# The second SwiGLU half step of a hybrid decoder: gate and up by seven products of block sums, down by pairs of tiles

## The chip, the cores and the metric

One core of a Trainium2 chip runs the whole program. The metric is the device time in microseconds (us) of one execution, as a median of several runs; the trace is that of one profiled execution. The engines are PE (TensorE, the matmuls; PEld its weight loads), DVE (VectorE), ACT (ScalarE), POOL (GpSimd) and SP (SyncE, which issues the DMA transfers here).

## The reference

The program is one step of a decoder layer over 1056 tokens (1024 of a prompt and 8 x 4 samples; 16 meta tokens more are carried through the first part). Of the layer only the end matters here:

```python
h = h + 0.5 * _swiglu(_rmsnorm(h, norm_ffn1), ...)            # first half step
...                                                           # GLA and S5 branches
h = h + merged @ p["w_out"]                                   # output projection
h = h + 0.5 * _swiglu(_rmsnorm(h, p["norm_ffn2"]), w_gate, w_up, w_down)   # second half step
# _swiglu(x) = (silu(x @ w_gate) * (x @ w_up)) @ w_down ; D_MODEL 1024, D_FF 2816
# then the final RMSnorm; _rmsnorm(x) = x * rsqrt(mean(x * x) + eps) * gain
```

All is float32.

## The kernel before

**Tiling.** Activations are feature-major: 128 features on the partitions, 8 feature tiles (k), tokens along the free axis. Tokens are cut into the chunks CH2 of 256, 384 and 416 columns. D_FF is 22 tiles of 128 (f tiles), taken in groups of 2, 4, 4, 4, 4 and 4 (FGROUPS). Weights come as tiles of [128, 1024], 512 KB each, in the order of use, from one array (`wst`).

**Products.** Weight and activation are each cut exactly into a high part of 12 bits and a rest, and three matmuls take the place of one: wh with xh (L702), wh with xl (L703), wl with xh (L704). `group()` does this for the 8 k tiles of one output tile and one chunk, 24 matmuls into one bank of PSUM. There are four banks named mm for the products and four named sm for small sums. `split()` cuts an activation: ACT copies the high part (L692), DVE or POOL subtracts it (L693).

**Weights.** The class `Weights` holds two rings: raw tiles as loaded by SP (2 buffers, wr) and split tiles (3 pairs, wh and wl). ACT copies the high part of a whole tile (L598), and DVE subtracts the rest (L610) some work later, in `lag()`. Tiles are split two ahead of their use.

**The second half step** is done by `ffn()`. Its gate and up tiles run tile by tile, and in each over the three chunks, 24 matmuls a group; only the first three tiles run chunk by chunk, so that they can start with the chunk that was normed first. An evicted gate is a Silu on ACT (L862). An evicted up is a product with it on DVE (L36) and a split: ACT the high part `ah` (L692), DVE the rest `al` (L693). Then `down` runs over 8 output tiles and three chunks, contracting over the f tiles of the group (4 x 3 = 12 matmuls), and DVE adds half of it to h (L52, the tile g). In the last group down runs chunk by chunk in the order 2, 1, 0, and the final norm of a chunk runs beside the next.

**The norm** (`Norm`) squares each finished tile of h on ACT (L778) and sums squares on POOL or DVE (nacc); `sums(c)` adds over features by matmul (L796) and takes an inverse root on DVE by 13 small instructions; `apply` spreads the root by matmul (L814) and scales h (L52), and splits the result into xh and xl.

**What sets the order.** All engines run in the order in which the code issues. Side work comes from generators: after each group `sch.slot()` runs one step of the ones that are queued, `sch.later(d, ...)` starts one d slots later, and `sch.drain()` runs all that is left at once. Ahead of the second half step stands `w_out` (output projection): chunks 0 and 1 tile by tile, then chunk 2, eight groups; the norms of chunks 0 and 1 are applied beside those.

## Time and profile before

| | |
|---|---|
| median of 3 runs | 2736.09 us (2735.72 to 2737.88) |
| span of the profiled execution | 2734.5 us |
| PE busy | 2663.9 us, 97% |
| DVE, ACT, POOL busy | 45%, 26%, 18% |
| last w_out matmuls, first matmuls of the second half step | 1951.63, 1951.82 us |
| last matmul of a product | 2721.16 us |

The times are those of one profiled execution, whose span is 1.6 us below the median of the runs. A row of the timeline gives the start, the duration, engine, line and operation, the tile written and those read, and in brackets the idle time ahead with what ended it. Matmuls overlap: a row's duration is longer than the distance to the next one, and it is the distance from start to start that adds up.

### The profile page before, as it was taken

What the parts mean: (1) busy time and instruction counts of PE and PEld (TensorE: products, weight loads), DVE (VectorE), ACT (ScalarE), POOL (GpSimd) and SP (SyncE); (2) the same over time, 40 slices, a digit from 0 to 9 for tenths busy, and PEclk for the clock granted to TensorE, in tenths of its full rate; (3) what the DMA queues carried; (4) which work ended last, traced back from release to release, by engine and by line L of the source; (5) the groups of instructions that cost most, each with busy time, mean ns of one, the idle gap of its engine ahead of it and who ended that gap; (6) DMA issues with size and microseconds to landing.
All of it is one profiled execution on the core that took longest, in us unless ns stands there. A gap on an engine that the chain in (4) does not pass through costs nothing. (4 is left out here: it accounts for less than half of the span.)

```text
span 2734.5 us, 41275 instructions
## 1 busy us (share of the span) xinstructions
PE 2663.9 (97%) x16796; PEld 2605.8 (95%) x16796; DVE 1231.5 (45%) x2677; ACT 712.2 (26%) x1302; POOL 482.6 (18%) x1006
## 2 busy tenths in 40 slices
PE   7999999999999899999999999999999999999998
PEld 7999999998999899999988989999999999999997
DVE  6545455664355777124455533253642323232325
ACT  4121212111233465334234312122412111212122
POOL 2000000677032343003123310001200000000002
PEclk8999999999999999999999999999999999999999
DMA  3111111442106576411211435343211111111111
GB/s 120 47 47 42 45 47 50 142 127 97 62 26 213 168 210 183 131 54 55 80 66 49 150 103 165 134 140 105 70 54 47 47 47 47 47 47 47 47 47 64
DMA packets 135790, 236.92 MB, mean 87 GB/s; under 512 B 21872, under 2 KB 100016, under 8 KB 134576
## 3 DMA queue, kind: packets, MB, share of 16 engines
q1 hardware_dynamic: 135600, 234.29, 26.2%
q8 instruction: 132, 2.16, 0.3%
q14 instruction: 58, 0.48, 0.1%
HBM read 180.40 MB, written 53.84 MB: 86 GB/s over the span
## 5 line engine op out<-in xcount | busy, mean ns | idle before, releaser
L702 PE MATMUL mm<-xh,wh 128*128 128x256 f32 (+3 forms) x3648 | 1194.2, 327 | 8.3 <-ACT xh L956 6.5
L704 PE MATMUL mm<-xh,wl 128*128 128x256 f32 (+3 forms) x3648 | 1186.5, 325 | 2.6 <-DVE wl L610 2.6
L703 PE MATMUL mm<-xl,wh 128*128 128x256 f32 (+3 forms) x3648 | 1184.4, 325 | 0.5 <-POOL xl L693 0.5
L702 PEld LDWEIGHTS mm<-xh,wh 128*128 128x128 f32 x3648 | 693.7, 190 | 18.5 <-ACT xh L956 6.5
L704 PEld LDWEIGHTS mm<-xh,wl 128*128 128x128 f32 x3648 | 693.0, 190 | 8.6 <-DVE wl L610 3.8
L703 PEld LDWEIGHTS mm<-xl,wh 128*128 128x128 f32 x3648 | 693.6, 190 | 7.9 <-POOL xl L693 1.6
L610 DVE TENSOR_TENSOR wl<-wr,wh 128x1024 fp32r<-128x1024 f32 x218 | 271.5, 1246 | 377.8 <-ACT wh L598 377.3
L598 ACT ACTIVATE wh<-wr 128x1024 fp32r<-128x1024 f32 x218 | 229.0, 1052 | 485.2 <-PE mm L703 371.5
L702 PE MATMUL mm<-ah,wh 128*128 128x256 f32 (+3 forms) x1008 | 327.0, 324 | 6.6 <-ACT ah L692 5.9
L703 PE MATMUL mm<-al,wh 128*128 128x256 f32 (+3 forms) x1008 | 327.1, 324 | 0.0
L704 PE MATMUL mm<-ah,wl 128*128 128x256 f32 (+3 forms) x1008 | 325.8, 323 | 0.0
L36 POOL TENSOR_TENSOR nacc<-nacc,nsq 128x384 f32<-128x384 f32 (+3 forms) x63 | 65.1, 1033 | 1051.5 <-ACT nsq L778 1047.2
L702 PEld LDWEIGHTS mm<-ah,wh 128*128 128x128 f32 x1008 | 190.1, 189 | 9.6 <-ACT ah L692 6.2
L703 PEld LDWEIGHTS mm<-al,wh 128*128 128x128 f32 x1008 | 189.9, 188 | 1.7 <-DVE al L693 0.4
L704 PEld LDWEIGHTS mm<-ah,wl 128*128 128x128 f32 x1008 | 190.1, 189 | 1.4
L692 ACT ACTIVATE ah<-at 128x256 fp32r<-128x256 f32 x132 | 66.1, 501 | 418.6 <-DVE at L36 418.6
L36 DVE TENSOR_TENSOR at<-mm,sg 128x256 f32<-128x256 f32 x132 | 69.3, 525 | 220.6 <-PE mm L704 195.1
L36 POOL TENSOR_TENSOR sg<-sg,root 128x384 f32<-128x384 f32 (+1 forms) x44 | 47.3, 1078 | 482.0 <-ACT sg L866 482.0
L52 DVE SCALAR_TENSOR_TENSOR g<-mm,g 128x256 f32<-128x256 f32 (+2 forms) x144 | 74.5, 522 | 128.4 <-PE mm L704 127.7
L52 DVE SCALAR_TENSOR_TENSOR h<-mm,h 128x256 f32<-128x256 f32 (+2 forms) x144 | 74.2, 525 | 73.2 <-PE mm L704 72.3
L693 DVE TENSOR_TENSOR al<-at,ah 128x256 fp32r<-128x256 f32 x132 | 70.3, 532 | 74.8 <-ACT ah L692 74.8
L49 POOL TENSOR_SCALAR rq<-rq,rq 128x1 f32<-128x1 f32 (+1 forms) x216 | 86.3, 400 | 21.7
(421 smaller groups left out, 2659.1 us busy)
## 6 DMA issues: line engine op xcount, KB each, us to landing
wr<-wst SPq DMA_DIRECT2D x220, 512.0 KB, 3.3
U<-ub SPq DMA_DIRECT2D x8, 584.0 KB, 4.7
yb<-ysb SPq DMA_DIRECT2D x64, 69.0 KB, 3.9
yt<-yb SPq DMA_DIRECT2D x8, 552.0 KB, 4.3
y<-y SPq DMA_DIRECT2D x8, 528.0 KB, 4.2
rd<-rot SPq DMA_DIRECT2D x8, 520.0 KB, 3.2
rot<-rd SPq DMA_DIRECT2D x8, 520.0 KB, 4.0
at<-Ad SPq DMA_DIRECT2D x32, 128.0 KB, 3.4
```

The lines of the kernel that those rows point to most:

```text
L36: (eng or self.nc.vector).tensor_tensor(out=out, in0=a, in1=b, op=op)
L49: (eng or self.nc.vector).tensor_scalar(out=out, in0=a, scalar1=s1, scalar2=s2, op0=op0, **kw)
L52: self.nc.vector.scalar_tensor_tensor(out=out, in0=a, scalar=s, in1=b, op0=op0, op1=op1)
L598: self.nc.scalar.activation(out=h, in_=r, func=AF.Copy)
L610: e.tensor_tensor(out=l, in0=r, in1=h.bitcast(FT), op=OP.subtract)
L692: act.activation(out=xh, in_=t, func=AF.Copy)
L693: (eng or v).tensor_tensor(out=xl, in0=t, in1=xh.bitcast(FT), op=OP.subtract)
L702: pe.matmul(p, wh[:, b], xh, start=(k == 0), stop=False)
L703: pe.matmul(p, wh[:, b], xl, start=False, stop=False)
L704: pe.matmul(p, wl[:, b], xh, start=False, stop=(k == nk - 1))
```

## The change

It replaces `ffn()` in the second half step; the first half step is as before.

**Gate and up.** Two f tiles (i rows of blocks), the two halves of the 8 k tiles, and two quarters of the tokens make a product of 2 x 2 by 2 x 2 blocks, which is done with seven products of sums of blocks in place of eight. The 1056 tokens are two halves p = 0, 1 of two quarters each, 264 columns a quarter. `variants(p, R)` makes the seven sums of normed activations for a half: per pair of k tiles (k, k + 4) four normed tiles (DVE), four subtractions (POOL), and seven splits (ACT copies, five DVE and two POOL subtractions). The sums of the first half are queued beside the last w_out chunk and finished by a drain; those of the second half are queued beside the first products. The class `Stream` loads the two weight tiles of a gate or up of two f tiles into the same raw ring of 2, and POOL forms four sums of 128 x 512; each of the seven operands is copied by ACT (L1668) and subtracted by DVE, two ahead of use, into a ring of 3. `unit()` runs the seven products: for each p 4 k tiles x 3 matmuls of 264 columns, accumulated into three banks a, c, b in the order "acbacaa". An output is complete after products 2, 4, 5 and 6 of the seven (counted from 0): ACT copies what has to be added later out of PSUM, DVE adds it.

**Order.** The plan begins with gate 0, up 0 and gate 1 on half 0 alone (g0, u0, g1), then the same on half 1, with the weights loaded and summed again, then down 0. From then on units cover both halves: u1, g2, d1, u2, g3, d2, ... u10, d10.

**Down** goes by pairs of f tiles: 8 output tiles x 3 parts of 352 tokens, 6 matmuls each. The last one goes chunk by chunk with the final norm beside it.

Around it, w_out and the merge ahead of it use chunks of 264, 396 and 396 tokens, h comes as one tile loaded after the merge, the stream of weights ends before the second half step, a small parameter load (pg) is made later, and a ring of small tiles (rq) has 3 buffers for 4.

```diff
-    n4 = Norm(tp, CH2, h, 32, out=A["o_y"], engs={0: (v,), None: (g,)})
-    wi = ffn(wi, CH2, h, n3.get, tp, n4, (2, 1, 0))
+    def variants(p, R):
...
+        for kp in range(4):
+            x11 = nrm(kp, 0)
+            x12 = nrm(kp, 1)
+            put(0, kp, x11, v)
+            o.sub(x11, x12, x11, g)
+            x22 = nrm(kp + 4, 1)
+            put(1, kp, x11, v)
+            o.sub(x12, x22, x12, g)
+            x21 = nrm(kp + 4, 0)
+            yield
+            put(4, kp, x22, v)
+            o.sub(x22, x22, x11, g)
+            put(2, kp, x21, v)
+            put(5, kp, x12, g)
+            o.sub(x21, x21, x22, g)
+            yield
+            put(3, kp, x22, v)
+            put(6, kp, x21, g)
+            yield
...
+    sch.later(1, lambda: n3.sums(0))
+    sch.later(3, lambda: n3.sums(1))
+    sch.later(4, lambda: sch.add(variants(0, SG[:, 0, 0:2])))
     for m in range(8):
         w_out(m, 2, wi + 8 + m)
-    n3.fin(2, 3)
+    wi += 16
+    n3.sums(2)
+    sch.drain()
...
+        def unit(self, key, i1, i2):
+            r = {}
+            lo, hi = slice(0, 512), slice(512, 1024)
+            def load():
+                r[0], r[1] = self.raw(i1), self.raw(i2)
+                r[2] = fw.tile([P, 512], FT, name="s1")
+                o.add(r[2], r[1][:, lo], r[1][:, hi], g)
+                o.sub(r[1][:, lo], r[0][:, lo], r[1][:, lo], g)
+            self.item(None, load)
+            self.item((key, 0), lambda: r[0][:, lo])
+            self.item(None, lambda: self.flush() or o.sub(r[0][:, lo], r[2], r[0][:, lo], g))
+            self.item((key, 1), lambda: r[2])
+            self.item((key, 2), lambda: r[0][:, hi])
+            self.item(None, lambda: self.flush() or o.sub(r[0][:, hi], r[0][:, hi], r[0][:, lo], g))
+            self.item((key, 3), lambda: r[0][:, lo])
+            self.item((key, 4), lambda: r[0][:, hi])
+            self.item((key, 5), lambda: r[1][:, lo])
+            self.item((key, 6), lambda: r[1][:, hi])
...
+        for i in range(7):
+            b = ws.get((x, i), num[0])
+            num[0] += 1
+            for p in ps_:
+                if FIRST[i]:
+                    bank[p, BANK[i]] = (ps_sm() if BANK[i] == "b" else ps_mm())[:, :HALF]
+                ps = bank[p, BANK[i]]
+                xh, xl = V[p][i]
+                for k in range(4):
+                    wh, wl = b[:, P * k:P * k + P], b[:, 512 + P * k:512 + P * k + P]
+                    pe.matmul(ps, wh, xh[:, k], start=FIRST[i] and k == 0, stop=False, skip_group_check=True)
+                    pe.matmul(ps, wh, xl[:, k], start=False, stop=False, skip_group_check=True)
+                    pe.matmul(ps, wl, xh[:, k], start=False, stop=(k == 3), skip_group_check=True)
+                if i == 0:
+                    copy(p, "p1", ps)
+                elif i == 1:
+                    copy(p, "p5", ps)
+                elif i == 2:
+                    out(p, 0, 0, ps, cp.pop((p, "p1")))
+                elif i == 3:
+                    copy(p, "u2", ps)
+                elif i == 4:
+                    out(p, 0, 1, ps, cp.pop((p, "u2")))
+                elif i == 5:
+                    out(p, 1, 1, ps, cp.pop((p, "p5")))
+                else:
+                    out(p, 1, 0, ps, None)
+                ws.flush()
+                sch.slot()
```

In `out` a gate is added on DVE where something is to be added and gets its Silu on ACT in place; an up is added and multiplied on DVE and split as before.

How this stands on the engines, at three places. ACT's instructions about the first products of the second half step, before (L598 are weight copies, L862 the first gates' Silus, nsq squares for the norm):

```order
L778 ACTIVATE nsq<-g_18499 128x416 [waits DVE_49,Activation_49,Pool_49]
L598 ACTIVATE wh<-wr 128x1024 [waits DMAHW0_49,PE_49]
L778 ACTIVATE nsq<-g_18499 128x416 [waits DVE_49,Pool_49]
L598 ACTIVATE wh<-wr 128x1024 [waits DMAHW1_49,PE_49]
L862 ACT_TABLE_LOAD
L862 ACTIVATE sg<-mm 128x256 [waits PE_49]
L692 ACTIVATE ah_19465<-at 128x256 [waits DVE_49]
```

and in the changed kernel (L705 are the high parts of the activation sums, L1668 the weight copies, L1749 the copy of the first product out of PSUM):

```order
L705 ACTIVATE xh_19016<-t 128x264 [waits DVE_49]
L705 ACTIVATE e_19020<-t 128x264 [waits Pool_49]
L705 ACTIVATE xl_19017<-t 128x264 [waits Pool_49]
L705 ACTIVATE e_19022<-t 128x264 [waits Pool_49]
L1668 ACTIVATE wv<-wr 128x512 [waits DMAHW1_49,PE_49]
L1668 ACTIVATE wv<-s_19488 128x512 [waits Pool_49]
L1668 ACTIVATE wv<-wr 128x512
L1749 ACTIVATE t<-mm 128x264 [waits PE_49,Activation_49]
```

The weight copies for the first product, which stood among the squares of w_out, now stand behind the last activation sum.

POOL at the same place. Before it has sums of squares of the last w_out chunk and rests of the normed chunks:

```order
L36 TENSOR_TENSOR nacc_19042<-nacc_19042,nsq 128x416 [waits Pool_49]
L693 TENSOR_TENSOR xl_19552<-at,xh_19551 128x416 [waits PE_49,Activation_49]
L693 TENSOR_TENSOR xl_19552<-at,xh_19551 128x416 [waits DVE_49,Activation_49]
L693 TENSOR_TENSOR xl_19552<-at,xh_19551 128x416 [waits Activation_49] x2
L36 TENSOR_TENSOR nacc_25224<-nacc_25224,nsq 128x416 [waits Activation_49]
```

The last of these rows is already that of the final norm; POOL has nothing between. After (s1 and wr are weight sums, t and L706 activation sums):

```order
L36 TENSOR_TENSOR s1_19488<-wr_19486 128x512 [waits DMAHW2_49,PE_49]
L36 TENSOR_TENSOR wr_19486<-wr_19484,wr_19486 128x512 [waits DMAHW4_49,DMAHW5_49,DMAHW3_49,DMAHW6_49,DMAHW1_49,DMAHW7_49,DMAHW0_49,Pool_49]
L36 TENSOR_TENSOR wr_19484<-s1_19488,wr_19484 128x512 [waits DMAHW5_49,DMAHW3_49,DMAHW7_49,DVE_49,Pool_49]
L36 TENSOR_TENSOR wr_19484<-wr_19484 128x512 [waits DVE_49,Pool_49]
L36 TENSOR_TENSOR t_19546<-t_19548,t_19546 128x264 [waits DVE_49]
L36 TENSOR_TENSOR t_19548<-t_19553,t_19548 128x264 [waits DVE_49,Pool_49]
L36 TENSOR_TENSOR t_19553<-t_19553,t_19546 128x264 [waits DVE_49,Pool_49]
L706 TENSOR_TENSOR e11_19481<-t_19548,e10_19480 128x264 [waits Activation_49]
L36 TENSOR_TENSOR t_19558<-t_19558,t_19553 128x264 [waits DVE_49,Pool_49]
L706 TENSOR_TENSOR e13_19483<-t_19558,e12_19482 128x264 [waits Activation_49]
```

POOL now makes weight sums throughout the stage, and in its beginning activation sums between them.

DVE in the middle of the stage, before, one up tile and its neighbours (L610 the rests of weights):

```order
L610 TENSOR_TENSOR wl<-wr,wh 128x1024 [waits DMAHW4_49,PE_49,Activation_49]
L36 TENSOR_TENSOR at<-mm,sg 128x256 [waits PE_49]
L693 TENSOR_TENSOR al_19774<-at,ah_19773 128x256 [waits Activation_49]
L36 TENSOR_TENSOR at<-mm,sg 128x384 [waits PE_49,Pool_49]
L693 TENSOR_TENSOR al_19805<-at,ah_19804 128x384 [waits Activation_49]
```

and after, from the second half of product 4 of u1 to the first of product 6 (wv the rests of weights; xh0_19014 is the tile that holds the gates; al the rest of the split output):

```order
L36 TENSOR_TENSOR t_20764<-mm_20683,t_20764 128x264 [waits PE_49]
L36 TENSOR_TENSOR t_20764<-t_20764,xh0_19014 128x264 [waits DVE_49]
L706 TENSOR_TENSOR al0_20628<-t_20764,ah0_20627 128x264 [waits Activation_49]
L36 TENSOR_TENSOR wv_20808<-wr_20768,wv_20808 128x512 [waits DMAHW3_49,Activation_49]
L36 TENSOR_TENSOR t_20680<-mm_20635,t_20680 128x264 [waits PE_49]
L36 TENSOR_TENSOR t_20680<-t_20680,xh0_19014 128x264 [waits DVE_49]
L706 TENSOR_TENSOR al1_20630<-t_20680,ah1_20629 128x264 [waits Activation_49]
L36 TENSOR_TENSOR t_20696<-mm_20650,t_20696 128x264 [waits PE_49]
L36 TENSOR_TENSOR t_20696<-t_20696,xh0_19014 128x264 [waits DVE_49]
L706 TENSOR_TENSOR al1_20630<-t_20696,ah1_20629 128x264 [waits Activation_49]
L36 TENSOR_TENSOR t_20858<-mm_20635,xh0_19014 128x264 [waits PE_49]
```

Where an output had two DVE instructions it now has three, and they follow one another with weight rests between; the last product has no addition.

## Rows read from the trace of the kernel before

**Rows 1.** The page: span, busy time by engine, chain that ended last by line.
```profile
span 2734.5 us, 41275 instructions
...
PE 2663.9 (97%) x16796; PEld 2605.8 (95%) x16796; DVE 1231.5 (45%) x2677; ACT 712.2 (26%) x1302; POOL 482.6 (18%) x1006
...
PE mm L704 9%; PE mm L702 9%; PE mm L703 9%; DVE g L52 0%; PE sm L796 0%; DVE nacc L36 0%; PE sm L814 0%; ACT nsq L778 0%; DVE wl L610 0%; POOL nacc L36 0%; POOLq L1614 0%; DVE rq L36 0%; DVE rq L52 0%; DVE rq L49 0%; DVEq L1614 0%
```

**Rows 2.** Windows, second half step: us, busy PE, PEld, DVE, ACT, POOL; clock, DMA.
```profile
1955.00:2721.00 766.00, 764.26 (x4769) 760.33 (x4769) 242.33 (x410) 143.25 (x228) 20.12 (x19) 1.00 0.14 47
```

**Rows 3.** Timeline of PE: the first matmuls of three consecutive groups.
```profile
2100.18 0.35 PE L702 MATMUL mm<-xh,wh 128*128 128x416 f32 x1
...
2104.71 0.28 PE L702 MATMUL mm<-xh,wh 128*128 128x256 f32 x1
...
2107.58 0.34 PE L702 MATMUL mm<-xh,wh 128*128 128x384 f32 x1
```

**Rows 4.** ACT's groups by form: count | busy us, mean ns | idle before.
```profile
L598 ACT ACTIVATE wh<-wr 128x1024 fp32r<-128x1024 f32 x218 | 229.0, 1052 | 485.2 <-PE mm L703 371.5 <-issue 107.3 <-PE mm L1334 4.0
...
L692 ACT ACTIVATE ah<-at 128x256 fp32r<-128x256 f32 x44 | 18.4, 418 | 76.9 <-DVE at L36 76.9
...
L692 ACT ACTIVATE ah<-at 128x416 fp32r<-128x416 f32 x22 | 12.2, 552 | 88.5 <-DVE at L36 88.5
...
L862 ACT ACTIVATE sg<-mm 128x256 f32<-128x256 f32 x22 | 8.5, 385 | 22.8 <-PE mm L704 22.8
```

**Rows 5.** Timeline of DVE and ACT: a weight's rest, the eviction of an up.
```profile
2660.12 1.23 DVE L610 TENSOR_TENSOR wl<-wr,wh 128x1024 fp32r<-128x1024 f32 x1 [9.74 <-ACT wh L598]
2661.43 0.42 DVE L36 TENSOR_TENSOR at<-mm,sg 128x256 f32<-128x256 f32 x1
2661.89 0.42 ACT L692 ACTIVATE ah<-at 128x256 fp32r<-128x256 f32 x1 [1.80 <-DVE at L36]
2662.34 0.43 DVE L693 TENSOR_TENSOR al<-at,ah 128x256 fp32r<-128x256 f32 x1 [0.48 <-ACT ah L692]
```

**Rows 6.** Timeline of POOL: operations on two operands, 256 and 416 columns.
```profile
1931.35 0.74 POOL L693 TENSOR_TENSOR xl<-at,xh 128x256 fp32r<-128x256 f32 x1 [2.31 <-ACT xh L692]
...
2683.10 1.08 POOL L36 TENSOR_TENSOR nacc<-nacc,nsq 128x416 f32<-128x416 f32 x1 [1.14 <-ACT nsq L778]
```

**Rows 7.** DMA issues, 2000 to 2735 us: count, KB each, us from issue to landing.
```profile
wr<-wst SPq DMA_DIRECT2D x58, 512.0 KB, 3.2
```

**Rows 8.** Timeline of the end: additions to h, last matmul, last square sum, last scaling.
```profile
2673.43 0.58 DVE L52 SCALAR_TENSOR_TENSOR g<-mm,g 128x416 f32<-128x416 f32 x1
...
2721.16 0.28 PE L704 MATMUL mm<-ah,wl 128*128 128x256 f32 x1
...
2722.48 0.42 DVE L36 TENSOR_TENSOR nacc<-nacc,nsq 128x256 f32<-128x256 f32 x1 [0.21 <-ACT nsq L778]
...
2727.38 3.22 DVE L52 SCALAR_TENSOR_TENSOR g<-g,par,sm 128x256 f32<-128x256 f32 x8 [1.38 <-PE sm L814]
```

**Rows 9.** Timeline of DVE: first and last of the 13 instructions of an inverse root.
```profile
2692.09 0.16 DVE L49 TENSOR_SCALAR rq<-sm 128x4 f32<-128x4 f32 x1 [0.96 <-PE sm L796]
...
2694.28 0.16 DVE L52 SCALAR_TENSOR_TENSOR rq<-rq,rq 128x4 f32<-128x4 f32 x1
```

**Rows 10.** Timeline of POOL and DVE in the S5 branch, 520 columns.
```profile
880.66 1.82 POOL L36 TENSOR_TENSOR sa<-rot,X 128x520 f32<-128x520 f32 x1
881.23 1.81 DVE L36 TENSOR_TENSOR sa<-rot,X 128x520 f32<-128x520 f32 x1
...
884.69 0.73 DVE L36 TENSOR_TENSOR sa<-sa 128x520 f32<-128x520 f32 x1
```

**Rows 11.** Windows in the S5 branch, columns as in rows 2.
```profile
890.00:892.00 2.00, 0.00 (x0) 0.00 (x0) 1.97 (x2) 0.09 (x1) 1.86 (x2) 0.84 0.29 86
...
896.00:898.00 2.00, 2.00 (x8) 2.00 (x7) 1.97 (x4) 0.00 (x0) 0.00 (x0) 0.50 0.71 248
898.00:900.00 2.00, 2.00 (x12) 2.00 (x12) 0.86 (x2) 0.00 (x0) 0.19 (x1) 0.95 0.00 0
```

More of the change, by code (lines that the diff above doesn't have):

```diff
@@ L652, in build @@
     xa = pool(ctx, "acts")
+    n_ffn = sum(2 * len(fs) + len(fs) for fs in FGROUPS)
+    W.end -= n_ffn
+    wctx = ctx.enter_context(ExitStack())
+    W.open(wctx, tc)
     class Sched:
@@ new lines, in build, with tt_, unit, out @@
+    ws.last = (len(plan) - 1, 3)
+    for x, (kind, n, ps_) in enumerate(plan):
+        gi, a, it, id_ = pairs[n]
+        if kind == "d":
+            ws.down(x, id_, (gi, a))
+        else:
+            e = int(kind == "u")
+            ws.unit(x, it + e, it + 2 + e)
+    SGs = SG
+    num = [0]
+    BANK = "acbacaa"
+    FIRST = (True, True, True, False, False, False, False)
+    aH = {}
+    def tt_():
+        return tp.tile([P, HALF], FT, name="t", bufs=TB)
+    def unit(x, kind, n, ps_):
+        bank, cp = {}, {}
+        if kind == "u" and n not in aH:
+            aH[n] = [[fa.tile([P, NT2], FR, name=f"a{i}{f}") for i in "hl"] for f in range(2)]
+        def out(p, f, i, ps, other):
+            s = SGs[:, p, 2 * f + i]
+            if kind == "g":
+                if other is not None:
+                    o.add(s, ps, other)
+                    act.activation(out=s, in_=s, func=AF.Silu)
+                else:
+                    act.activation(out=s, in_=ps, func=AF.Silu)
+                return
+            if other is not None:
+                o.add(other, ps, other)
+                o.mul(other, other, s)
+            else:
+                other = tt_()
+                o.mul(other, ps, s)
+            q = slice(HALF * (2 * p + i), HALF * (2 * p + i + 1))
+            split(aH[n][f][0][:, q], aH[n][f][1][:, q], other)
+        def copy(p, name, ps):
+            cp[p, name] = t = tt_()
+            act.activation(out=t, in_=ps, func=AF.Copy)
+        for i in range(7):
[5 more added lines that the diff above has]
+                ps = bank[p, BANK[i]]
+                xh, xl = V[p][i]
+                for k in range(4):
[15 more added lines that the diff above has]
+                    out(p, 1, 1, ps, cp.pop((p, "p5")))
+                else:
+                    out(p, 1, 0, ps, None)
+                ws.flush()
+                sch.slot()
@@ new lines, in down @@
+    def down(x, n):
+        for q in range(4):
+            b = ws.get((x, q), num[0])
+            num[0] += 1
+            for j in range(2):
+                m = 2 * q + j
+                for t0, nn in CHD:
+                    ps = down_group(n, b, j, t0, nn)
+                    o.stt(H[:, m, t0:t0 + nn], ps, 0.5, H[:, m, t0:t0 + nn], OP.mult, OP.add)
+                    ws.flush()
+                    sch.slot()
+        del aH[n]
+    for x, (kind, n, ps_) in enumerate(plan[:-1]):
+        if x == 3:
+            sch.drain()
+        if x == 0:
+            hi = [xa.tile([P, 3, 4, HALF], FR, name=f"x{i}2") for i in "hl"]
+            parts = [y[:, j] for y in hi for j in range(3)] + [q4(e_(i, FR)) for i in range(6, 14)]
+            V[1] = [tuple(parts[2 * i:2 * i + 2]) for i in range(7)]
+            sch.add(variants(1, SG[:, 1, 0:2]))
+        if kind == "d":
+            down(x, n)
+        else:
+            unit(x, kind, n, ps_)
@@ new lines, in build @@
+    x, n = len(plan) - 1, plan[-1][1]
+    h = [H[:, :, t0:t0 + nn] for t0, nn in CHM]
+    n4 = Norm(tp, CHM, h, 32, out=A["o_y"], engs={0: (v,), None: (g,)}, acc=lambda c, i: e_(6 + c), sq=sq_)
+    bs = []
+    for z, c in enumerate((2, 1, 0)):
+        t0, nn = CHM[c]
+        for m in range(8):
+            if z == 0 and m % 2 == 0:
+                bs.append(ws.get((x, m // 2), num[0]))
+                num[0] += 1
+            pd = down_group(n, bs[m // 2], m % 2, t0, nn)
+            o.stt(h[c][:, m], pd, 0.5, h[c][:, m], OP.mult, OP.add)
+            ws.flush()
+            n4.add(c, m)
+            sch.slot()
+        n4.fin(c, *((1, 2) if z < 2 else (2, 1)))
@@ L1517, in build @@
     sch.flush()
-    assert wi == len(A["order"])
     ch2.close()
```

181 lines of the change are left out of this document (149 added, 32 removed).

## The prediction

> **What bounds the kernel now.** I read the busy times first, then the chain that ended last: PE is busy 97% of the span, and the chain consists almost wholly of the three matmul lines, with small shares of anything else [rows 1]. The reader should see that nothing but columns through PE is worth removing. The stretch that the change rewrites is the second half step, 1955 to 2721 us: PE is busy 764.26 of 766.00 us there, at full granted clock, while DVE, ACT and POOL are busy 242, 143 and 20 us [rows 2]. So this stage is pure PE work with three nearly idle engines, and the question is whether the work put on them stays hidden.
>
> **What the change removes.** Matmuls follow each other at a pace set by their columns: 24 of 256 columns take 2107.58 - 2104.71 = 2.87 us, 119.6 ns each; 24 of 416 take 4.53 us, 188.8 ns each [rows 3]. The line between these is 0.432 ns a column plus 8.9 ns, so 264 columns cost 123.1 ns, 352 cost 161.1, 396 cost 180.1. Before, gate and up are 44 f tiles x 8 k tiles x 3 products of (256+384+416) columns: 1056 triples x (119.6+174.0+188.8 = 482.4 ns) = 509.4 us. After, 22 units x 7 products x 2 halves x 12 matmuls x 123.1 ns = 455.0 us. Down stays at 528 triples x 0.483 us = 254.7 us. (1584 triples x 0.4824 = 764.1 us, which is the 764.26 of [rows 2].) **Gain: 54.4 us.**
>
> **What it adds: prices of the new steps.** A 1024-column weight copy on ACT takes 1.05 us, a 416-column split 0.55, one of 256 0.42, so 512 columns take 0.63 and 264 take 0.43; a Silu of 256 columns out of PSUM takes 0.39, taken for the PSUM copies too [rows 4]. On DVE a subtraction takes 0.43 at 256 columns and 1.23 at 1024: 0.44 at 264, 0.69 at 512 [rows 5]. On POOL 256 columns take 0.74 and 416 take 1.08: 0.75 at 264, and at 512, outside these rows, 1.25 to 1.3 [rows 6]. A 512 KB weight load lands in 3.2 us [rows 7].
>
> **S, the entry.** The sums of activations for the first half of the tokens run one step to a slot from the fifth group of the last w_out chunk on. When PE ends w_out, one k pair of four and a third of the next are done. sums(2) stands ahead of the rest: addition to h 0.58, square 0.55, POOL's sum 1.08, 0.96 until DVE has it, then the inverse root on DVE from 2692.09 to 2694.44, 2.35 us [rows 4, 6, 8, 9]: 5.5 us, or 7.8 with three POOL subtractions queued ahead. One k pair is 9 DVE, 6 POOL and 7 ACT instructions (4.0, 4.5, 3.0 us) that depend on each other across engines; following the arrows of the code I get 6.1 us where engines overlap, 7.5 where DVE and POOL disturb each other in part. 2.67 pairs: 16.3 to 20.0. Behind all of it stands, on ACT in order, the copy of the first weight (L1668, 0.63), then its DVE half (0.69), then product 0 (12 x 0.123 = 1.48). Product 0 so ends 24.6 to 30.6 us after w_out instead of 1.5, and the next waits 1 to 2 more for POOL's weight sum. Before, the first gate group began at once, since its chunk was normed earlier. S is 24 to 31, I take **28**, nearer the top, as both engines run dense there.
>
> **H1, the second half's sums beside the first 14 products.** Three products on half the tokens take PE 3 x 1.48 = 4.43 us. Beside them go one k pair and three weight operands: POOL 6 x 0.75 + (12/7) x 1.25 = 6.6; DVE 9 x 0.44 + 3 x 0.69 + about 1 of evictions + small gaps = 7.0; ACT 7 x 0.43 + 3 x 0.63 + 3 x 0.39 = 6.1. All exceed PE. Four k pairs: at least 4 x (7.0 - 4.43) = 10; with DVE and POOL strictly in turns 4 x (13.6 - 4.43) = 37. The rows on which POOL and DVE worked side by side on operands of SBUF show 1.81 and 1.82 us for a 520-column instruction on each, against 0.73 on DVE by itself [rows 10]: taking turns is real. I take **22**, between, since a good part of both engines' time here is waiting for others, which needs no turn.
>
> The Trainium skill, SBUF — State Buffer, section "Who interferes with whom", says that a DVE instruction with two SBUF inputs contends with a GpSimd instruction that reads SBUF, under an exclusive lock that fully blocks the later one. The trace agrees with its sign and size (1.81 against 0.73 us). It speaks against this change, which puts both kinds on both engines at once; held to the letter it makes H1 37 instead of 22, which is rival B.
>
> **H2, four more boundaries of units on half the tokens** (u0 to g1, g1 to g0, g0 to u0, u0 to g1). The ring of raw weights has two buffers, so a unit's second tile is asked for only when the last copy and subtraction of the unit before it are through, in its product 4: 2.75 us (gate) or 4.1 us (up, whose evictions take DVE) after that product's start. Then load 3.2, POOL's sum 1.25, ACT 0.63, DVE 0.69: product 1 of the next unit can start 8.5 to 8.8 or 9.9 to 10.2 us after, against 4 x 1.48 = 5.9 on PE. The loss is 2.6 to 2.9 twice and 4.0 to 4.3 twice: 14, and 22 if POOL and DVE queue once more at each; **16**. With all tokens a product is twice as long and the same chain is hidden.
>
> **U, nine full boundaries from an up unit to the next gate unit.** An eviction of up is add 0.43, multiply 0.43, 0.48 waiting for ACT's half of the split, subtraction 0.43 [rows 5]: 1.78 us per half product against 1.48 on PE, with weight subtractions of 0.69 between. From product 4 on all of them come in a row; product 6 goes into the bank that product 5's addition still reads. With DVE at 1.78 + 0.69 + 1.78 + 0.69 + 0.43 = 5.4 after the first of these, where PE would start product 6 at 4.43, the loss is 1.0, and the other half adds 0.3 to 1.3. So 1.3 to 2.3, 1.8 each: **16**. Before, a group of 24 matmuls hides one such eviction (4.53 against some 1.9).
>
> **u10 to the last down and the tail.** The same late evictions before the last down, with no gate unit between: **3.5** (2.5 to 4). The last down has 16 x 6 x 0.1801 + 8 x 6 x 0.1231 = 23.2 us of matmuls for the final norm to hide behind, where before the last group had 46.3. DVE has 24 evictions (16 x 0.56 + 8 x 0.42 = 12.3), three inverse roots (7.0), 24 applications (about the same each, 3.22 for the last eight: 12.2), 8 sums of the last chunk's squares (3.4) and 2.8 of weights: 37.7, or 14.5 over. Of that the last root and the last applications, 2.35 + 3.22 = 5.6, lay behind the last matmul before, too, in the 13 us from there to the end [rows 8, 9]. That leaves **9** (6 to 11).
>
> **Sum.** Span 2734.5 [rows 1] - 54.4 + 28 + 22 + 16 + 16 + 3.5 + 9 = 2774.6. The median of the runs is 1.6 above that span, so **2776 us**, 1.5% slower. All low ends together (24, 10, 12, 12, 2.5, 6) give 2748, all high ends (31, 37, 22, 21, 4, 11) 2807. The new order of chunks in w_out and merge (264, 396, 396) carries the same columns and costs nothing; 1.5 us would be the price of one stall there.
>
> **Rivals.** *A, faster:* the preparation stays ahead of PE. For it: ACT, DVE and POOL are idle 81, 68 and 97% of this stage [rows 2], w_out's last chunk is 8 groups of 4.3 us in which the sums could start, and the nine full units have the engines below PE's time (DVE 17.7 of 20.7 us). Then S is 5, H1 and H2 9 together, U 5, tail 6: 25 in all, 2707 us. Against it: the steps are one to a slot, and slots end with w_out. It decides if PE's first matmul of the second half step comes within 5 us of the end of w_out. Chance 0.12. *B, much slower:* DVE and POOL strictly in turns. H1 37 and S 32 instead of 22 and 28, and in full units DVE 17.7 + POOL 5.0 = 22.7 against 20.7, up to 2 more at some boundaries: 2776 + 15 + 4 + about 6 = 2801. Against it: half of DVE's instructions there read PSUM or are waits. Chance 0.11. *C, the clock:* after an idle PE the granted clock was 0.50, which is 1.2 GHz, while PE was already fully busy, before it rose to 0.95 [rows 11]. PE idle a third of the time in the half-token units could keep it low: a unit there takes 20.7 us instead of 10.3, hidden in H1 by the other engines, not in H2, 4 x 10.3 = 41 instead of 16: 2801. Against it: stops here are short, 3 to 4 us, between stretches of several us of work. Chance 0.07. *D, the change doesn't do what it says:* shorter matmuls could lose to a fixed cost. Excluded for size: 256 columns already run at 119.6 ns [rows 3]; weight loads lie beside them.
>
> **How the numbers follow.** The forecast's own sum has 0.66, with 2748 to 2807; A has 0.12, B 0.11, C 0.07, and 0.04 lies between the forecast and A, about the old time. A range of 2738 to 2810 leaves out A, and the upper parts of B and C, some 0.2. Within 0.2%, 5.5 us, about what a measurement of this kernel can tell from no change: 0.05. Faster 0.12, slower 0.83.
>
> **What would show it.** Right, if in the new profile (1) 264-column matmuls start 123 ns apart inside a product; (2) PE stands still 20 us or more behind w_out, released by ACT's or DVE's activation sums; (3) the first 14 products take some 62 us rather than 41; (4) PE waits 3 to 4 us for the weight operand of product 1 in the half-token units; (5) each full up unit loses near 2 us waiting for DVE's evictions; (6) the end lies some 22 us after the last matmul, where it was 13. Wrong, if PE is above 95% busy in the first 100 us of the second half step (S and H1 fall, the time nears A), or if POOL and DVE double each other's instructions throughout (B).

## The result and the profile after

The changed kernel takes 2805.81 us (median; 2804.43 to 2806.79) against 2735.9: ratio 1.0256, 95% interval 1.0241 to 1.027. The forecast was 2776, 1.5% slower, in a range of 2738 to 2810. Sign and range held; of the slowdown, 70 us, the forecast had 40. The total by itself decides little: it lies nearer to the 2801 of the rivals B and C than to the forecast's own 2776, and close to the 2807 that all its high ends give together. What held and what did not is read from the places.

The page of the changed kernel, busy time by engine, beside [rows 1]:

```profile
PE 2644.4 (94%) x17344; PEld 2579.8 (92%) x17344; DVE 1469.4 (52%) x3162; ACT 834.7 (30%) x1667; POOL 649.1 (23%) x1142
```

PE has 19.5 us less to do and the span is 69.5 us longer (2804.0). The chains of the two pages can't be compared: the one before reaches back over only 27% of its span, about the second half step, and the one after over nearly the whole program.

The windows of the changed kernel, cut at the first matmul of each piece of the plan: entry, g0, u0, g1 on half 0, then g0, u0, g1 on half 1, all from d0 to u10, and the last down. Columns as in [rows 2]:

```profile
1953.40:1981.15 27.75, 1.97 (x10) 1.79 (x9) 16.79 (x42) 8.95 (x23) 16.59 (x20) 0.54 0.00 0
1981.15:2011.61 30.46, 17.07 (x99) 15.74 (x99) 16.91 (x29) 12.98 (x29) 18.09 (x18) 0.72 0.10 36
2011.61:2035.87 24.26, 15.94 (x85) 15.03 (x85) 17.08 (x33) 10.87 (x27) 11.21 (x13) 0.71 0.14 44
2035.87:2057.09 21.22, 15.33 (x86) 14.62 (x86) 7.35 (x13) 7.30 (x17) 8.88 (x10) 0.74 0.15 49
2057.09:2070.46 13.37, 11.26 (x86) 10.86 (x86) 8.45 (x10) 6.73 (x14) 4.38 (x4) 0.96 0.23 80
2070.46:2088.90 18.44, 12.72 (x86) 11.72 (x85) 11.01 (x16) 6.98 (x15) 7.75 (x6) 0.91 0.18 59
2088.90:2101.38 12.48, 10.73 (x85) 10.34 (x85) 7.24 (x12) 6.29 (x13) 3.61 (x3) 1.00 0.14 43
...
2101.38:2745.82 644.44, 624.80 (x4634) 620.84 (x4633) 376.65 (x684) 198.08 (x439) 102.53 (x76) 1.00 0.15 48
2745.82:2804.00 58.18, 35.34 (x190) 33.35 (x188) 35.38 (x101) 13.64 (x28) 14.75 (x14) 0.78 0.23 83
```

The reader sees a bad start (each half-token unit, a gate or up on one half of the tokens, has 10.3 us of matmuls), a long middle with PE near full, and a bad end. PE's waits by releaser, 1940 us to the end (total, times, longest):

```profile
PE mm L1760 <- DVE t L36: 28.3, 22, 4.8
PE mm L1760 <- ACT wv L1668: 25.9, 5, 20.7
PE mm L1760 <- DVE xh L36: 15.8, 4, 11.2
PE sm L811 <- POOL e L36: 11.2, 3, 5.1
PE mm L1762 <- DVE wv L36: 7.0, 8, 1.2
```

Before, PE was idle 1.7 us from 1952 us to its last product matmul. The sum by places, each worked out from the starts of first matmuls (whole units against 84 or 168 matmuls of 123.1 ns, which is what the forecast counted):

| place | forecast | measured |
|---|---|---|
| gain of the seven products | -54.4 | -54.4, and 2.4 more in g and d units |
| w_out ends later (1953.33 against 1951.82) | 0 | +1.5 |
| S: standstill 27.8, product 0 5.75 for 1.48 | +28 | +32 |
| H1: g0 and u0, rest of 54.7 over 20.7 | +22 | +30 |
| H2: next four half units, 65.5 over 41.4 | +16 | +24 |
| U: u1 to u9, 207.3 over 186.1 | +16 | +21 |
| u10 (1.2) and a wait in d10 (1.8) | +3.5 | +3 |
| T: last down, 58.2 to the end, less those 1.8, with 23.2 of matmuls; before 64.6 with 46.3 | +9 | +15 |
| sum | +40.1 | +70 (span: +69.5) |

The places are those of one trace for each kernel. In seven other traces below, with the same w_out, w_out ends between 1950.7 and 1954.1, so the 1.5 us of its row are no more than executions differ by.

The 5.75 us up to product 1 are not a wait:

```profile
1981.15 0.59 PE L1760 MATMUL mm<-xl,wv 128*128 128x264 f32 x1 [20.71 <-ACT wv L1668]
...
1984.36 2.68 PE L1545 MATMUL sm<-ident,rq 128*128 128x120 f32 x14
1986.90 0.37 PE L1760 MATMUL mm<-xh,wv 128*128 128x264 f32 x1
```

Product 0 takes 3.2 us, 9 of its 12 matmuls at 220 ns from start to start, the low level of the clock (granted 0.53 in these 5.75 us). Behind it PE's order has 14 small matmuls that spread the root for the second half's activation sums, 2.5 us. These belong with H1 rather than with S.

### The profile page after: what moved, and what is told of

Same layout as the page of the kernel before. It is cut to its first block, busy times and chain, and to the rows that moved or that the text cites. A ratio compares the mean times of both kernels' runs of the same rounds, so it can differ in the third digit from the quotient of the medians.

```text
span 2804.0 us, 43738 instructions
## 1 busy us (share of the span) xinstructions
PE 2644.4 (94%) x17344; PEld 2579.8 (92%) x17344; DVE 1469.4 (52%) x3162; ACT 834.7 (30%) x1667; POOL 649.1 (23%) x1142
## 4 chain that ended last, share of the span: by engine, by line
PE 76%; DVE 9%; POOL 4%; issue 3%; ACT 3%; DMA 1%; SPq 0%; POOLq 0%; DVEq 0%; ACTq 0%
PE mm L715 16%; PE mm L716 16%; PE mm L717 16%; PE mm L1760 3%; PE mm L1762 3%; PE mm L1761 3%; PE mm L1787 3%; PE mm L1788 3%; PE mm L1789 3%; POOL rot L36 1%; DVE t L36 1%; PE mm L1348 1%; PE mm L1350 1%; PE mm L1349 1%; DVE wv L36 1%
## 5 line engine op out<-in xcount | busy, mean ns | idle before, releaser
L715 PE MATMUL mm<-xh,wh 128*128 128x256 f32 (+5 forms) x2592 | 855.8, 330 | 9.8 <-ACT xh L971 6.1
L716 PE MATMUL mm<-xl,wh 128*128 128x256 f32 (+5 forms) x2592 | 849.4, 328 | 1.0 <-POOL xl L706 0.5
L717 PE MATMUL mm<-xh,wl 128*128 128x256 f32 (+5 forms) x2592 | 846.2, 326 | 1.6 <-DVE wl L618 1.6
L715 PEld LDWEIGHTS mm<-xh,wh 128*128 128x128 f32 x2592 | 494.2, 191 | 20.0 <-ACT xh L971 6.1
L716 PEld LDWEIGHTS mm<-xl,wh 128*128 128x128 f32 x2592 | 494.6, 191 | 7.4 <-POOL xl L706 1.6
L717 PEld LDWEIGHTS mm<-xh,wl 128*128 128x128 f32 x2592 | 494.3, 191 | 6.7 <-DVE wl L618 2.3
L52 DVE SCALAR_TENSOR_TENSOR h<-mm,h 128x352 f32<-128x352 f32 (+5 forms) x408 | 210.7, 524 | 167.9 <-PE mm L1789 93.7
L1760 PE MATMUL mm<-e,wv 128*128 128x264 f32 x616 | 180.3, 293 | 45.2 <-DVE t L36 28.3
L1762 PE MATMUL mm<-e,wv 128*128 128x264 f32 x616 | 179.4, 291 | 3.3 <-DVE wv L36 3.3
L1761 PE MATMUL mm<-e,wv 128*128 128x264 f32 x616 | 178.2, 289 | 0.0
L1787 PE MATMUL mm<-ah,wv 128*128 128x352 f32 (+2 forms) x516 | 168.0, 326 | 1.8 <-ACT ah L705 1.8
L1668 ACT ACTIVATE wv<-wr 128x512 fp32r<-128x512 f32 x193 | 120.2, 623 | 159.9 <-PE mm L1789 149.5
L1788 PE MATMUL mm<-al,wv 128*128 128x352 f32 (+2 forms) x516 | 167.6, 325 | 0.0
L1789 PE MATMUL mm<-ah,wv 128*128 128x352 f32 (+2 forms) x516 | 167.5, 325 | 0.0
```

The costliest lines, as they stand in the source:

```text
L52: self.nc.vector.scalar_tensor_tensor(out=out, in0=a, scalar=s, in1=b, op0=op0, op1=op1)
L715: pe.matmul(p, wh[:, b], xh, start=(k == 0), stop=False)
L716: pe.matmul(p, wh[:, b], xl, start=False, stop=False)
L717: pe.matmul(p, wl[:, b], xh, start=False, stop=(k == nk - 1))
L1760: pe.matmul(ps, wh, xh[:, k], start=FIRST[i] and k == 0, stop=False, skip_group_check=True)
L1761: pe.matmul(ps, wh, xl[:, k], start=False, stop=False, skip_group_check=True)
```

## The experiments

All times are medians of four runs beside runs of the kernel before on the same chip (2735.8 to 2737.9). "Faster" is against the changed kernel's 2805.81, which was measured on another occasion; as the medians of the kernel before differ by up to 2 us between occasions, and four runs of one kernel spread over 2 to 8 us, gains of 2 or 3 us are not told apart from none.

**Weight sums later in POOL's queue.** The largest single stop is in g0, between products 5 and 6. The timeline of the changed kernel there:

```profile
2002.93 1.26 POOL L36 TENSOR_TENSOR s<-wr 128x512 f32<-128x512 f32 x1 [4.09 <-DMA wr<-wst]
...
2006.26 0.42 ACT L705 ACTIVATE xh<-t 128x264 fp32r<-128x264 f32 x1 [6.01 <-POOL t L36]
2006.71 0.62 DVE L706 TENSOR_TENSOR xl<-t,xh 128x264 fp32r<-128x264 f32 x1 [5.60 <-ACT xh L705]
...
2008.27 0.42 DVE L36 TENSOR_TENSOR xh<-mm,t 128x264 f32<-128x264 f32 x1
...
2008.83 0.56 PE L1760 MATMUL mm<-e,wv 128*128 128x264 f32 x1 [11.25 <-DVE xh L36]
```

POOL stands 4 us at a weight sum whose tile is still coming, in front of the activation subtractions; ACT waits for those, DVE for ACT, and the addition that frees PE's bank (2008.27) stands behind that in DVE's queue. `e_late` takes POOL's weight sums a product later:

```diff
+
+            def sums():
                 o.add(r[2], r[1][:, lo], r[1][:, hi], g)
                 o.sub(r[1][:, lo], r[0][:, lo], r[1][:, lo], g)
+                self.flush()
+                o.sub(r[0][:, lo], r[2], r[0][:, lo], g)
+                return r[2]
             self.item(None, load)
             self.item((key, 0), lambda: r[0][:, lo])
-            self.item(None, lambda: self.flush() or o.sub(r[0][:, lo], r[2], r[0][:, lo], g))
-            self.item((key, 1), lambda: r[2])
+            self.item((key, 1), sums)
```

> Edit: POOL's four weight sums of a unit are issued one product later (with the second operand's copy), so that activation subtractions stand ahead of them in POOL's queue; the loads are issued as before. Theory Q (queue): in the first two half-token units POOL stands at a weight sum whose tile is still on its way, with the activation subtractions, DVE and PE behind it; then g0 and u0 together fall from 54.7 us to 36 to 45, and the total by 10 to 18 us, to 2788 to 2796. Rival W (work): the stage is bound by how much DVE and POOL have to do, whatever the order; then g0 and u0 stay within 3 us of 54.7 and the total within 4 us of 2805.8.

2792.85, so 13.0 faster, within the range of theory Q, but not where Q put it: g0 and u0 still take 52.3 us (25.3 and 27.0). That stop fell from 11.25 to 5.05 us, and other waits, for the now later weights, took most of it back. As an account of H1, Q falls. Most of the gain is in the up units of the middle, 21.9 us each in place of 23.0 (10.6 us in nine units; 3.0 lie ahead of down 0), and its reason shows in the next experiment.

**Up's rests on POOL.** `e_u_pool`:

```diff
-            split(aH[n][f][0][:, q], aH[n][f][1][:, q], other)
+            split(aH[n][f][0][:, q], aH[n][f][1][:, q], other, g if len(ps_) == 2 else None)
```

> Edit: in units over both halves the rest of an up's split is subtracted on POOL in place of DVE. Theory D: the full up units last 23.0 us instead of 20.5 because DVE comes late with the addition that frees a bank; then u1 to u9 fall to 20.5 to 21.2 us and the total by 16 to 22, to 2784 to 2790. Rival: POOL's subtractions slow DVE's instructions on two operands as much as they relieve it; units stay above 22.3 and the total within 6 us of 2805.8.

2784.4: 21.4 faster, as theory D has it. u1 takes 20.91 us, and the whole middle is PE's again:

```profile
2100.07:2724.07 624.00, 622.08 (x4635) 620.43 (x4634) 341.21 (x607) 199.71 (x440) 170.31 (x155) 1.00 0.16 50
```

What made DVE late is seen in the changed kernel at u1's products 5 and 6:

```profile
2139.27 0.43 DVE L706 TENSOR_TENSOR al<-t,ah 128x264 fp32r<-128x264 f32 x1 [0.49 <-ACT ah L705]
...
2143.31 0.36 PE L1760 MATMUL mm<-e,wv 128*128 128x264 f32 x1 [1.14 <-DVE t L36]
2143.92 1.28 POOL L36 TENSOR_TENSOR s<-wr 128x512 f32<-128x512 f32 x1 [16.46 <-DMA wr<-wst]
2144.12 1.37 DVE L706 TENSOR_TENSOR al<-t,ah 128x264 fp32r<-128x264 f32 x1 [0.49 <-ACT ah L705]
2145.28 1.35 POOL L36 TENSOR_TENSOR wr<-wr 128x512 f32<-128x512 f32 x1
2145.42 0.42 DVE L36 TENSOR_TENSOR t<-mm,t 128x264 f32<-128x264 f32 x1
2145.87 1.05 DVE L36 TENSOR_TENSOR t<-t,xh 128x264 f32<-128x264 f32 x1
...
2145.89 0.39 PE L1760 MATMUL mm<-e,wv 128*128 128x264 f32 x1 [0.89 <-DVE t L36]
```

One part of the 2.3 us is the train of evictions that the forecast had (1.14). The other is POOL: while its weight sums run, DVE's subtraction takes 1.37 us instead of 0.43, and the multiplication 1.05; the addition with an operand in PSUM keeps 0.42. In `e_late` that POOL sum begins one eviction later, behind the addition for which the first half of product 6 waits, and about half is saved. `e_u_pool` takes work off DVE as well as out of POOL's way, and does not tell the two apart.

The Trainium skill, SBUF — State Buffer, section "Who interferes with whom", has it that a DVE instruction with two SBUF inputs contends with a GpSimd instruction that reads SBUF, and that one with at most one SBUF input, outside the 2-port perf modes, does not. The trace agrees on both (1.37 and 1.05 against 0.43 without POOL; 0.42 for the addition beside POOL).

**The entry.** `e_entry` makes the first two weight operands ahead of the drain and puts `n3.sums(2)` behind it:

```diff
-    n3.sums(2)
-    sch.drain()
...
+    ws.advance(1)
+    ws.flush()
+    sch.drain()
+    n3.sums(2)
```

> Edit: the first two weight operands are copied and subtracted ahead of the drain of the activation sums, and the sums of squares of the last chunk come behind the drain. Theory S: the standstill behind w_out consists of things in front of product 0 that it doesn't need; PE's first product moves from 28 to 15 to 19 us behind w_out and the total falls by 8 to 12, to 2794 to 2798. Rival: the chain of activation sums sets the pace anyway; product 0 is early but products 1 to 6 wait as long as before, and the total falls by less than 4.

2809.64: no gain, a miss of both. PE's first product came later, at 1984.48, since the matmul of the sums of squares (L811) now stood in PE's own order ahead of product 0, and its POOL sum behind all activation sums. PE's waits from 1950 us on:

```profile
PE sm L811 <- POOL e L36: 34.7, 3, 28.5
```

**Two steps to a slot.** `e_dense` starts the sums of the first half earlier and steps them twice a slot:

```diff
-    sch.later(3, lambda: n3.sums(1))
-    sch.later(4, lambda: sch.add(variants(0, SG[:, 0, 0:2])))
+    sch.later(2, lambda: n3.sums(1))
+    sch.later(3, lambda: sch.add(variants(0, SG[:, 0, 0:2])))
     for m in range(8):
         w_out(m, 2, wi + 8 + m)
+        if m >= 2:
+            sch.slot()
```

> Edit: the activation sums of the first half start one slot earlier beside the last w_out chunk and run two steps to a slot from its third group on. Theory S: the standstill behind w_out is what the one-step-to-a-slot pace left undone (2.7 of 4 k pairs); PE's first product moves from 28 to 9 to 15 us behind w_out's end, and the total falls by 12 to 18, to 2788 to 2794. Rival: DVE and POOL are then busy so densely that w_out's additions come late and PE loses in w_out what it gains behind it; total falls by less than 6.

2802.97, 2.8 faster, which the spread of its runs (2798.67 to 2805.61) does not tell from none: the rival. The last w_out chunk takes 43.2 us from its first matmul to its last instead of 37.3, since weight copies and rests come late behind the sums, and then PE stands 14.6 us at the sums of squares, which wait for POOL. The first product comes 16.6 us behind w_out instead of 28.0, and g0 then takes 35.5 us instead of 30.5. What a quicker pace takes off the entry comes back in w_out and g0, which speaks for the length of the sums on POOL and DVE as the limit.

**The activation sums on DVE.** `e_vardve`:

```diff
-            o.sub(x11, x12, x11, g)
+            o.sub(x11, x12, x11)
...                      # the other three likewise
```

> Edit: the four subtractions by which a k pair's activation sums are formed go to DVE in place of POOL, in both halves; the splits and the weight sums stay. Theory P (a chain through POOL): each sum waits for a slow POOL instruction between DVE's and ACT's, so the chain gets shorter although DVE has four more instructions; entry 28 to 21 to 25 us, g0 and u0 together from 54.7 to 38 to 46, total lower by 12 to 22, 2784 to 2794. Rival W (DVE's work bounds): DVE goes from 9 to 13 instructions a k pair, g0 and u0 together rise to 58 to 64, the entry stays, total 2808 to 2818.

2791.33: 14.5 faster, inside the range of theory P for the total. The entry falls from 28.0 to 23.1 us (w_out's last matmul starts at 1951.87 in this run, the first product at 1974.98), g1 from 21.2 to 15.3; but g0 and u0 give back only 2.9 (25.5 and 26.3). So P is right for the entry, neither P nor W for H1, and g1 is a gain that neither named. Windows of entry, g0, u0 in this run, the first cut where the changed kernel's was:

```profile
1953.40:1974.98 21.58, 1.05 (x8) 0.97 (x9) 19.92 (x53) 9.08 (x23) 5.84 (x7) 0.59 0.00 0
1974.98:2000.48 25.50, 18.64 (x98) 17.51 (x99) 19.18 (x35) 12.87 (x29) 11.49 (x10) 0.70 0.14 42
2000.48:2026.82 26.34, 16.84 (x85) 15.61 (x85) 24.20 (x45) 11.91 (x30) 7.84 (x8) 0.69 0.12 40
```

DVE is now busy 19.9 of these 21.6 us and 24.2 of 26.3 in u0: it is nearly full there, where in the changed kernel DVE and POOL were busy between 46 and 70% of these stretches.

**Without the second half's sums.** `e_novar1` puts `V[1] = V[0]` in place of the second call of `variants`.

> Leaves out the activation sums of the second half of the tokens; its products read the first half's instead. What g0 and u0 then lose against 10.3 us each is the price of weights alone. Theory (both Q and W): g0 and u0 fall from 54.7 us to 26 to 30, and the total by 25 to 30, to 2776 to 2781. Rival C (clock): if the low clock after the entry is what costs most, PE stays at 220 ns a matmul through these units and they keep above 40 us; total within 15 of 2805.8.

2780.65: 25.2 faster, as expected; g0 and u0 take 31.3 us (16.7 and 14.6), a little above the 26 to 30 expected. So of their 54.7 us 23.4 are the activation sums. All six half units still take 92.7 over 62.0 us, 31 us without those sums. The expectation called this the price of weights alone, and the trace shows it to be more than that. Rows of the changed kernel, g1 on half 0 and u0 on half 1:

```profile
2041.01 0.46 PE L1760 MATMUL mm<-xh,wv 128*128 128x264 f32 x1 [2.66 <-ACT wv L1668]
2042.87 0.59 PE L1762 MATMUL mm<-xh,wv 128*128 128x264 f32 x1 [1.17 <-DVE wv L36]
...
2054.55 0.36 PE L1760 MATMUL mm<-e,wv 128*128 128x264 f32 x1 [2.06 <-DVE xh L36]
...
2086.13 0.56 PE L1760 MATMUL mm<-e,wv 128*128 128x264 f32 x1 [3.94 <-DVE t L36]
```

The first two are waits for product 1's weights. The last two are product 6, which goes into the bank that DVE is still evicting product 5 from: on half the tokens the two follow each other directly. Every half unit in both traces stops there. From start to start of PE's matmuls, what exceeds 123.1 ns a step, in us:

| | weights | DVE's and ACT's evictions | steps at the slow pace, near 220 ns | rest, small matmuls with it |
|---|---|---|---|---|
| changed kernel, g0 and u0 on half 0 | 6.1 | 17.0 | 6.7 | 4.3 |
| changed kernel, the next four | 7.9 | 9.1 | 6.3 | 0.8 |
| `e_novar1`, g0 and u0 on half 0 | 1.2 | 4.8 | 3.1 | 1.6 |
| `e_novar1`, the next four | 9.1 | 7.7 | 2.7 | 0.5 |

So weights are 10 of the 31 us that half-token units pay without activation sums, and evictions, nearly all ahead of product 6, are 12.

**The clock.** `e_warm` puts 140 useless matmuls of 264 columns behind `n3.sums(2)`.

> Edit: 140 matmuls of 264 columns with no use are put on PE behind the sums of squares of the last chunk, so that PE works through the entry and the granted clock stays at its high level until the first product. Theory C (clock): the low clock, 220 ns a matmul in several products of g0, u0 and g1, costs 8 to 12 us; total 2794 to 2798. Rival: those products wait for operands anyway, the slow matmuls lie in waits; total within 4 us of 2805.8, or a little above it if the useless matmuls end late.

2805.83 (2804.09 to 2809.81): the rival's total. Windows of the entry, g0, u0:

```profile
1953.40:1979.87 26.47, 20.89 (x148) 20.68 (x149) 15.55 (x40) 8.31 (x22) 16.01 (x19) 0.87 0.00 1
1979.87:2010.22 30.35, 16.16 (x98) 14.92 (x99) 17.48 (x29) 12.98 (x29) 18.09 (x18) 0.79 0.11 36
2010.22:2034.48 24.26, 14.30 (x86) 13.40 (x85) 17.08 (x33) 10.82 (x27) 11.45 (x13) 0.78 0.14 44
```

The granted clock is 0.87 in the entry instead of 0.54, but 0.79 and 0.78 instead of 0.72 and 0.71 after it: it did not stay at its high level, and product 0 still runs at 220 ns. Of the steps at that pace g0 keeps all (25 for 24), u0 has 28 for 45, g1 21 for 42. u0 takes what it took, so its slow matmuls lie in waits. g1 takes 19.6 us instead of 21.2, but g1 on half 1 takes 15.5 instead of 12.5, with 20 slow steps for 2. So a faster clock in part of the stage does not change the total; what the low clock costs in g0, and in the stage as a whole, was not tested.

**The tail.** `e_tail` issues a chunk's sums of squares three groups after it instead of one (`n4.fin(c, 3, 2)` for `(1, 2)`). Rows of the changed kernel:

```profile
2776.42 1.87 PE L811 MATMUL sm<-one,e 128*128 128x1 f32 x8 [4.10 <-POOL e L36]
...
2782.48 2.24 DVE L52 SCALAR_TENSOR_TENSOR h<-h,par,sm 128x396 f32<-128x396 f32 x4 [0.49 <-PE sm L829]
...
2785.32 2.23 DVE L52 SCALAR_TENSOR_TENSOR h<-h,par,sm 128x396 f32<-128x396 f32 x4
...
2791.07 1.41 PE L811 MATMUL sm<-one,e 128*128 128x1 f32 x6 [4.96 <-DVE e L36]
```

> Edit: in the last down the sums of squares of a finished chunk are issued three groups later instead of one. Theory T: PE stands 2.1 and 4.1 us in its own order at those sums, which wait for POOL; the last down takes 58 us from its first matmul to the end, and falls to 50 to 54, total 2798 to 2802. Rival: DVE's work (additions, roots, scalings) sets the end, PE's stops lie beside it; the last down keeps 57 to 59 us, total within 2 of 2805.8.

2801.39: 4.4 faster, inside the range for the total. The last down takes 54.8 us for 58.2, which is a little above the 50 to 54 expected, and PE's stops at POOL's sums there fall from 6.2 to 1.9 us. They are real and worth about half of what T missed. What holds the rest was not taken apart by a run. The rows show one part: the eight scalings of the chunk before (4.5 us) stand in DVE's queue ahead of the last chunk's additions and squares, and PE waits 5.0 us for those (4.96 in the last row), as it still does in `e_tail` (5.1).

**g1 once for all tokens.** `e_plan` orders g0, u0 on half 0, g0, u0 on half 1, then g1 whole.

```diff
-            plan += [("g", 0, (0,)), ("u", 0, (0,)), ("g", 1, (0,)), ("g", 0, (1,)), ("u", 0, (1,)), ("g", 1, (1,)), ("d", 0, None)]
+            plan += [("g", 0, (0,)), ("u", 0, (0,)), ("g", 0, (1,)), ("u", 0, (1,)), ("g", 1, (0, 1)), ("d", 0, None)]
...
-        if x == 3:
+        if x == 2:
```

> Edit: the first gate of the second pair (g1) is done once for all tokens behind g0, u0, g0, u0, in place of once in each half; weights of one unit are loaded and summed once less. Theory H2 (each unit on half the tokens pays for its weights' chain of load, POOL, ACT, DVE): g1 and its second pass, 33.7 us together with their waits, become one unit of 20.5 to 23, while u0 pays 0 to 4 for activation sums that had g1 as cover; total lower by 6 to 12, 2794 to 2800. Rival: the waits are those of the activation sums and only move ahead, to the drain before the second half; total within 4 of 2805.8.

2800.4: 5.4 faster. g1 whole takes 22.6 us for 33.7 in two halves, as expected; but the second g0 takes 19.6 instead of 13.4 (and u0 15.7 instead of 18.4): part of what g1 paid is what the activation sums leave over, and it moves to the next unit, as the rival had it. The result lies between the two expectations, just outside H2's.

**Together.** `c_all` has e_u_pool, e_vardve, e_tail and e_plan; `c_all_late` also e_late.

> Four edits together: up's rests on POOL in full units, the four sums of a k pair on DVE, the final norm's sums two groups later, g1 once for all tokens. If their places are separate, as the theory has it, the gains add: 21.4 + 14.5 + 4.4 + 6 to 12 less than 2805.8 give 2754 to 2760. Rival: with POOL and DVE shared out anew they collide elsewhere; then less than 35 us is gained, above 2770. In either case the kernel before (2736) stays ahead, by the weights' chain in the half-token units and the entry.

> The four edits of the run before and the later weight sums. Theory: what later weight sums gained by themselves (13.0 us) was nearly all in the up units over both halves, 1.1 us each, where they keep a weight rest out of DVE's way; with up's rests on POOL that is gained already, so this run lies within 5 us of the one with four edits. Rival: POOL's queue still holds the activation sums up in the half-token units; another 8 to 13 us.

2758.2 and 2757.88. Singly the four gained 21.4 + 14.5 + 4.4 + 5.4 = 45.7, together 47.6: their places are separate. The later sums add nothing (0.3), as expected, but not for the reason given: in the traces u1 to u9 fall by another 4.1 us in sum, to 20.5 each, and the half-token units with g1 take 3.1 more, so that two effects cancel. Against the kernel before, c_all is still 1.0077 (1.0062 to 1.0092). Two stretches of it:

```profile
1955.00:2100.00 145.00, 99.09 (x632) 94.96 (x631) 103.34 (x196) 58.82 (x135) 47.66 (x40) 0.81 0.14 44
2100.00:2707.00 607.00, 605.00 (x4525) 603.35 (x4524) 329.54 (x586) 196.26 (x434) 165.54 (x151) 1.00 0.15 49
```

From 2100 us to the last down PE is idle 2 us of 607: there the seven products keep what they save. In the 145 us ahead of that PE is idle 46.

`c_dense` adds two steps to a slot from the fifth group on, and the first weights ahead of the remaining sums:

> The four edits of c_all; the activation sums of the first half run two steps to a slot from the fifth group of the last w_out chunk on, and the first two weight operands are made ahead of the sums that remain. With two steps to a slot alone the entry did not get shorter, since POOL, with four subtractions a k pair, was the engine that lagged, and PE stood at the sums of squares behind POOL's queue. Theory: with these on DVE the work can lie beside w_out; PE's first product moves from 24 to 11 to 16 us behind w_out's end, the total from 2758.2 to 2745 to 2751. Rival: DVE then keeps w_out's additions and weight rests waiting by as much; total within 4 us of 2758.2. Either way it stays behind the kernel before.

2759.23: the rival's total, but not its cause. The last w_out chunk takes 37.3 us as in c_all, so w_out was not held up; but the first product comes only 2.8 us earlier behind it (20.3 for 23.1), since PE waits 18.2 us at the sums of squares (L811) for POOL, and g0, entered early, takes 28.8 us instead of 25.5. No version was found that beats the kernel before.

## Why the prediction was right, and where it was short

- **Gain.** Right: a gate unit over all tokens takes 20.47 us, 121.8 ns a matmul against the 123.1 worked out from [rows 3].
- **S.** Right in place and, for the standstill itself, in size: 27.8 for 28, the row of copies and sums in the order that the rows of ACT had shown. e_vardve shows the chain through POOL to be 4.9 us of it. What makes it 32 are 1.7 us by which product 0 is slower than the 1.48 in the sum, and 2.5 of small matmuls for the second half's sums, which no term had. How the entry could be hidden stays open; three attempts moved the wait.
- **H1.** Right in sign, and inside 10 to 37, but not for the reason that set its middle. The forecast bounded it by work (POOL, or DVE and POOL in turns). e_novar1 shows the activation sums to cost 23.4 us, their small matmuls with them; relieving POOL (e_vardve) or reordering its queue (e_late) takes off 3 and 2. Whether what remains is work or the coupling of two chains in three ordered queues was not settled: with POOL relieved DVE is near full in u0, and without that neither engine is. Sign (3) of the forecast has a slip: the first 14 products have 20.7 us of matmuls, so that H1 makes it 43 rather than 21, and not 62 rather than 41; measured are 54.7.
- **H2.** Mis-sized, 24 for 16; that it comes near the upper end of 22 is luck. The wait of a half unit for its weights, the only cause that the term counted, is there but is 7.9 us, 4.3 of them in g1 on half 0, the one unit of the four that shows the 3 to 4 us of sign (4), and 9.1 in e_novar1. The term left out the wait ahead of product 6 for DVE's eviction, which the forecast had for full up units alone (U): 9.1 us here, 7.7 in e_novar1. The slow pace is 6.3 more. In e_novar1, where no activation sums run, the four units take 61.4 over 41.4 us; with them a remainder reaches into g1, which the forecast took to end in u0: g1 takes 21.2 us with them and 16.2 without, and 3.7 of these 5 us are slow pace.
- **U.** Right in mechanism, 21 for 16, 2.3 a unit at the upper end of 1.3 to 2.3. The missing part, as far as the rows and e_late show, is POOL's weight sum, which stretches DVE's instructions just there. The forecast knew the pair of rows that shows this [rows 10] and used it in its own sum for H1 alone; only rival B had it in full units.
- **T.** Mis-sized most for its size, 15 for 9. The term counted DVE's work and put it all behind the last matmul (sign 6: 22 us from there to the end); measured are 18.2, for 13.3 before. The larger part lies ahead of it: the term left out that PE itself runs in order. The sums of squares are PE's too, and behind POOL's additions, 1.0 to 1.25 us each, PE stands 6.2 us, for 1.5 before (e_tail, 4.4 back); and 25 product matmuls there run at the slow pace, 3 us longer in sum.
- **Rivals.** A fell: PE began 28 us behind w_out, not 5. B: DVE and POOL hold each other up in U (1.37 for 0.43 us); H1, at 30, lies between the forecast's 22 and B's 37, and no run says how much of it is turns. C: the clock fell as described, to 0.54 in the entry and 0.7 for the next 76 us. 135 of the 504 matmuls of the half-token units run at the slow pace, 13 us longer in sum; e_warm took 20 of these away and the total stayed. How much of the 13 us a high clock throughout would give back stays open.

The common fault: each term was priced for one cause, the engine or the chain that was thought to bound its place, and what else stops PE there was left out: other queues, the bank of product 6, the low clock. That made every large term too small and none too big. The total stayed inside the range because the range was as wide as all high ends together.

## What to carry to other kernels

A saving on the bound engine that is paid with preparation on three others is worth what its steady state keeps, less what its first and last pieces cost, where nothing lies ahead to hide behind: here 57 us less 21 in the up units, against 32 + 30 + 24 + 15 = 101 at entry, half-token units and end. Where a stage hands operands through several in-order engines, look at what stands in each queue ahead of the instruction that frees a bank. If DVE is late beside POOL, move the instructions with two operands in SBUF away from POOL's busy moments or onto POOL; the latter, which also takes work off DVE, gave 21 us here.
